# Attention's projections by halves of the heads, half of them between the heads; head norms' roots by Newton steps

## The chip, the cores and the metric

One core of one Trainium2 chip runs the whole program. The metric is the device time of one execution in microseconds (us). The engines are TensorE (PE in the rows; PEld is its weight load), VectorE (DVE), ScalarE (ACT), GpSimd (POOL) and SyncE (SP), which here only issues DMAs. TensorE's clock has two levels, 1.2 and 2.4 GHz; the rows give the granted clock as a share of the higher one.

## The reference, cut to what matters

Two layers over 256 latent and 256 context tokens of width 1024. Layer 0 is a gated convolution and a dense SwiGLU. Layer 1, where the change is, is differential attention and then 8 experts.

```python
q, k, v = split(a @ w_qkv, 3)          # latent tokens; the context needs only k and v
q = rms_norm(q.reshape(.., 16, 64), q_g); k = rms_norm(k.reshape(.., 16, 64), k_g)
q, k = rope_2d(q), rope_2d(k)          # latent tokens alone; context without rope
p = softmax(q @ k.T / 8)               # 16 half-heads, keys: latent and context
w = p[:, 0] - lam * p[:, 1]            # pairs of half-heads: 8 heads
o = rms_norm(w @ v, sub_g) * (1 - lam_init)
h = h + g1 * (o @ w_out)               # then the experts
```

## The kernel before, in words

**Matrix products.** Values are fp32. Each operand is split into a high and a low part (`hi`, `lo`), and a product is three TensorE matmuls (`mm3`: hi by hi, hi by lo, lo by hi). Tokens lie in four blocks of 128: blocks 0 and 1 are latent, 2 and 3 context. The activations' parts are `ah[k]` and `al[k]`, k = 0 to 7 over the depth of 1024.

**Weights.** They come by DMA in units of 1 MB (128 x 2048, four k steps of 512 columns each) into three raw buffers (`rw`, class `Loads`). Class `Parts` turns a unit into its parts: a cast on ScalarE (`wh`), then a subtraction on VectorE (`wl`). There are three slots for parts. `pump` converts what has arrived as long as a slot is free; `release` and `give` free the slots of units that are used up, and convert the next. 512 columns of the three matrices (two units) are numbered n: 0 and 1 are q, 2 and 3 are k, 4 and 5 are v. The even n are heads 0 to 3, the odd ones heads 4 to 7.

**Order.** Nothing is scheduled by a compiler: each engine works its instructions in the order in which the program issues them. What stands behind a waiting instruction on its engine waits too.

**Projections.** `group(n, pr, ws, new)` makes the 512 columns n for two token blocks (2pr and 2pr+1) in turns: at each of eight k steps one product (three matmuls) for the one block, one for the other. q needs one group, k and v two each. The first q group (n = 0) lies at the end of layer 0; in its midst stands `then()`, which reads the last mean, and `modulate`, which makes `ah` and `al` of the context blocks. Then `order` runs n = 1, 2, 3 and 4, that is all of q and k and half of v. Between the products of a group stands the head norm of the group before: `qk_norm` (square on ScalarE, sum per half-head on VectorE as `qr`, square root on ScalarE, reciprocal on VectorE, then the scaling `qx`, and rope in `qz` and `qy`), `qk_end` (the sum of the rope's parts), and `flip` (four transposes on TensorE into a PSUM bank, copied by ScalarE to `qT` or `kT`). `rows` makes three further rows that the end of the layer needs. Two banks of PSUM hold a group, and seven are there in all.

**Attention.** Sixteen steps m, one for each pair of a head and a latent block (`heads16`; before: block 0 with heads 0 to 7, then block 1). A step has `scores` (two matmuls into `sc`), `top` (the maxima `mx` on VectorE), `soft` (two exponentials `e` on ScalarE), for head m-1 `weigh` (VectorE, `zr` and `e`), for m-2 `turn` (four transposes into the one bank of `psw`, the tile `wt`, copied by ScalarE to `wT`), for m-3 `value` (four matmuls into `o`; the rows count each matmul of `scores` and `value` twice). With the first six heads `filler` runs the other half of v (n = 5), three k steps a head, two products each, in the two banks of `psf` (tile `mm`). Behind head 6 the slots of the weights are set free, and memory that is done with is given to further weights (`held.close`, pool `more`). `subnorm(t, ..)` and `sub_t(t, ..)` norm and transpose block t's outputs, and `outp` multiplies them with `w_out`; block 0 does so at steps 11 to 18, and block 1 after the loop.

Of the kernel before, what the change touches and what calls it, by code (L numbers as in the profile page):

```python
# [13 lines left out]
BF16 = mybir.dt.bfloat16  # L14
AF = mybir.ActivationFunctionType
# [4 lines left out]
P = 128  # L20
# [109 lines left out]
def backbone(ctx: ExitStack, tc: tile.TileContext, i, out, stage=9):  # L130
# [17 lines left out]
    units = [i["w0"][u] for u in range(49)] + [i["w1"][u] for u in range(16)]  # L148
# [475 lines left out]
    def group(n, pr, ws, new):  # L624

        ps = [new() for _ in range(2)]
        for k in range(KT):
            if len(ws) == k // 4:
                ws.append(parts.unit())
            wh, wl = ws[k // 4]  # L630
            c = slice(k % 4 * T2, (k % 4 + 1) * T2)
            for p, t in zip(ps, (2 * pr, 2 * pr + 1)):
                tk = slice(t * P, (t + 1) * P)
                mm3(p, ah[k][:, tk], al[k][:, tk], wh[:, c], wl[:, c], k == 0, k == KT - 1)
            yield ps

    for k, q0 in enumerate(group(0, 0, [], bank)):
        if k == 1:
            parts.pump(1)
        elif k == 2:  # L640
            jobs = then()
        elif k == 5:
            parts.give(1)
            modulate(jobs)
# [22 lines left out]
    pq = proj.enter_context(tc.tile_pool(name="qkv", bufs=1, side="right", reuse_waits="tile"))  # L667
# [4 lines left out]
    def qk_norm(ps, t, is_k):  # L672
        sq = pq.tile([P, T2], F32, name="qsq")
        A.activation(sq, ps, AF.Square)
        r = sm.tile([P, 8], F32, name="qr")
        V.tensor_reduce(r, heads(sq), axis=AX.X, op=OP.add)
        A.activation(r, r, AF.Sqrt, bias=eps, scale=1.0 / 64)
        V.reciprocal(r, r)
        x = pq.tile([P, T2], F32, name="qx", bufs=4)
        V.tensor_tensor(out=heads(x), in0=heads(ps), in1=r[:, :, None].to_broadcast([P, 8, 64]), op=OP.mult)  # L680
        if t >= 2:
            V.tensor_tensor(out=heads(x), in0=heads(x), in1=qkg[:, None, 64:].to_broadcast([P, 8, 64]), op=OP.mult)
            return x
        z = pq.tile([P, T2], F32, name="qz", bufs=2)
        xs = x.rearrange("p (h r b j) -> p h r b j", h=8, r=2, b=2)
        zs = z.rearrange("p (h r b j) -> p h r b j", h=8, r=2, b=2)
        rp = rope[:, is_k, 1, t].rearrange("p (r b j) -> p r b j", r=2, b=2)
        for r2 in range(2):
            for b in range(2):
                V.tensor_tensor(out=zs[:, :, r2, b], in0=xs[:, :, r2, 1 - b],  # L690
                                 in1=rp[:, None, r2, b].to_broadcast([P, 8, 16]), op=OP.mult)
        y = pq.tile([P, T2], F32, name="qy", bufs=2)
        V.tensor_tensor(out=heads(y), in0=heads(x), in1=rope[:, is_k, 0, t, None].to_broadcast([P, 8, 64]), op=OP.mult)
        return x, y, z

    def qk_end(a):
        if isinstance(a, tuple):
            x, y, z = a
            V.tensor_tensor(out=x, in0=y, in1=z, op=OP.add)
            return x  # L700
        return a

    def flip(x, t, dst):
        pt = bank()
        for j in range(4):
            PE.transpose(pt[:, j * P:(j + 1) * P], x[:, j * P:(j + 1) * P], ident)
        A.copy(dst[:, :, t * P:(t + 1) * P], pt.rearrange("p (n t) -> p n t", n=4))

# [28 lines left out]
    order = [(1, 0), (2, 0), (2, 1), (3, 0), (3, 1), (4, 0), (4, 1)]  # L737
    prev, flips, extra = (0, 0, q0), deque(), rows()
    ws = []
    for n, pr in order:  # L740
        if pr == 0:
            parts.release()
            parts.holding = n > 1
            ws = []
        xs = []
        for k, ps in enumerate(group(n, pr, ws, bank)):
            pn_, ppr, pps = prev
            if pn_ < 4:
                if k in (1, 2):
                    xs.append(qk_norm(pps[k - 1], 2 * ppr + k - 1, pn_ > 1))  # L750
                elif k in (3, 4):
                    xs[k - 3] = qk_end(xs[k - 3])
                    flips.append((xs[k - 3], 2 * ppr + k - 3, qT[pn_] if pn_ < 2 else kT[pn_ - 2]))
            elif k in (1, 2):
                A.copy(vv[pn_ - 4][2 * ppr + k - 1], pps[k - 1])
            if k > 5 and (len(flips) > 2 or pr and n == 4):
                flip(*flips.popleft())
            if k == 5 and pr:
                parts.give(1)
            if k in (3, 5) and n > 1:  # L760
                next(extra, None)
        prev = n, pr, ps
    for t in range(2):
        A.copy(vv[0][2 + t], ps[t])
    proj.close()
# [7 lines left out]
    onh, onl = (aw.tile([P, 2, 8, P], F32R, name=f"on{n}") for n in range(2))  # L773
# [3 lines left out]
    heads16 = [(h, t) for t in range(2) for h in range(8)]  # L777
# [74 lines left out]
    def filler():  # L852
        parts.release(1)
        parts.holding = True
        ws = []
        for pr in range(2):
            for k, ps in enumerate(group(5, pr, ws, lambda: psf.tile([P, T2], F32, name="mm"))):
                if k == 2:
                    parts.pump(1)
                yield  # L860
            for t in range(2):
                A.copy(vv[1][2 * pr + t], ps[t])

# [24 lines left out]
    fill, zs = filler(), {}  # L888
    out0 = None
    more = ExitStack()  # L890
    for m in range(19):
        if m < 16:
            scores(m)
        if 0 <= m - 3:
            value(m - 3)
        if 0 <= m - 2 < 16:
            turn(m - 2)
# [6 lines left out]
        if m < 6:  # L904
            for _ in range(3 if m < 5 else 2):
                next(fill, None)
        if m == 6:
            parts.release(1)
            held.close()
            pm = more.enter_context(tc.tile_pool(name="more", bufs=1, reuse_waits="tile"))  # L910
            parts.free.extend(part_slots(pm, 1, "x"))
            parts.last_use, xlo = parts.free[-1]
            parts.holding = True
            nh, nl = ([pm.tile([P, D], F32R, name=n), parts.last_use[:, c * D:(c + 1) * D]] for c, n in enumerate(("nh", "nl")))
            small = routing(pm)
            oh = [pm.tile([P, 2, P], F32R, name=f"oh{t}") for t in range(2)]
        if m in (7, 8, 9):
            parts.pump(1)
        if m == 11:
            subnorm(0, 0, 8)  # L920
        if m == 13:
            sub_t(0, 0, 4)
        if m == 14:
            sub_t(0, 4, 8)
        if m == 14:
            wo = [parts.unit() for _ in range(4)]
            out0 = [psf.tile([P, T2], F32, name="mm") for _ in range(2)]
        if m > 14:
            outp(out0, 0, m - 14 - 1)

        loads.free.extend({11: ada_slots[:1], 14: [flat], 15: ada_slots[1:] + later[:1], 18: later[1:]}.get(m, []))
# [5 lines left out]
    for h in range(18 - 14, 8):  # L937
# [398 lines left out]
```

## Time and profile before

| | |
|---|---|
| Median of 3 runs | 1669.6 us (1669.21 to 1669.99) |
| Profiled execution: its own time | 1667.59 us |
| Its span | 1665.3 us |
| TensorE busy | 1600.8 us, 96% of the span |
| VectorE, ScalarE, GpSimd busy | 80%, 53%, 1% |
| Layer 0 up to the first q | 0 to 612 us |
| q, k and half of v | 612 to 721 us |
| The sixteen heads | 721 to about 801 us |
| `subnorm`, output product, residual, routing | about 801 to 845 us |
| Experts | 845 to 1665 us |

Times in the trace count from the start of the span. A row of a timeline has the start, the time of one instruction (or of several alike that follow each other, with their count behind an x), engine, line, operation, what it writes and reads, and sizes. In square brackets stands how long the engine had been idle before it, and which engine's work ended that. For the matmuls the duration is modelled, so the distance of two starts says more than the duration of one.

### The profile page before, as it was taken

The numbers are of one execution on the slowest core, as the hardware profiler recorded it, in microseconds if no ns is written. First come the engines' busy times: TensorE is split into PE (matmuls) and PEld (weight loads), VectorE is DVE, ScalarE is ACT, GpSimd is POOL, SyncE is SP. The second block draws the span as 40 slices with busy tenths as digits, with TensorE's granted clock in tenths as the row PEclk, the third lists the DMA queues.
The fourth block names the chain that finished last, engine by engine and source line by source line (L and its number), as shares of the span: only waits on it lengthen the run. The fifth ranks groups of instructions, "written<-read, shape, count | busy, mean of one in ns | idle before, by whom it ended". The sixth has DMA issues, their size and how long they took to land. (4 is left out here: it accounts for less than half of the span.)

```text
span 1665.3 us, 20172 instructions
## 1 busy us (share of the span) xinstructions
PE 1600.8 (96%) x7415; PEld 1285.0 (77%) x7415; DVE 1328.9 (80%) x1886; ACT 885.5 (53%) x1241; POOL 13.1 (1%) x29
## 2 busy tenths in 40 slices
PE   8799899999999999997979999999999999999997
PEld 7587688888888887864768887888778887788886
DVE  5888887667658668536678898989989898998986
ACT  3222244222212244346557767777667776777774
POOL 0000000000001000000000000000000000000000
PEclk9999999999999999998979999999999999999999
DMA  9345534445547423212269988999889998899980
GB/s 357 106 175 199 186 109 167 152 149 180 177 165 273 168 84 119 102 51 101 102 237 361 366 331 324 350 350 374 313 336 356 356 346 323 331 365 348 357 339 28
DMA packets 55724, 400.30 MB, mean 240 GB/s; under 512 B 6449, under 2 KB 6481, under 8 KB 7105
## 3 DMA queue, kind: packets, MB, share of 16 engines
q1 hardware_dynamic: 55298, 398.50, 64.4%
q8 instruction: 60, 0.98, 0.2%
q0 software_dynamic: 320, 0.44, 0.2%
q14 instruction: 46, 0.38, 0.1%
HBM read 397.87 MB, written 1.05 MB: 240 GB/s over the span
## 5 line engine op out<-in xcount | busy, mean ns | idle before, releaser
L83 DVE TENSOR_TENSOR wl<-rw,wh 128x1024 fp32r<-128x1024 f32 (+1 forms) x211 | 321.9, 1561 | 98.1 <-ACT wh L79 97.6
L79 ACT CAST wh<-rw 128x1024 fp32r<-128x1024 f32 (+1 forms) x209 | 267.8, 1314 | 65.7 <-PE mm L174 57.4
L173 PE MATMUL mm<-ah,wh 128*128 128x512 f32 (+1 forms) x576 | 223.1, 387 | 7.9 <-ACT ah L313 7.3
L175 PE MATMUL mm<-ah,wl 128*128 128x512 f32 (+1 forms) x576 | 222.1, 386 | 5.0 <-DVE wl L83 5.0
L174 PE MATMUL mm<-al,wh 128*128 128x512 f32 (+1 forms) x576 | 222.4, 386 | 0.1
L253 DVE SCALAR_TENSOR_TENSOR junk<-ra,cb 128x1024 bf16<-128x1024 f32 x136 | 166.3, 1223 | 3.3
L175 PE MATMUL y<-wh,hl 128*128 128x512 f32 x352 | 141.6, 402 | 3.9 <-DVE hl L1132 3.8
L173 PE MATMUL h<-wh,xl 128*128 128x512 f32 x352 | 143.2, 407 | 0.0
L173 PE MATMUL h<-wh,xs 128*128 128x512 f32 x352 | 142.8, 406 | 0.0
L173 PE MATMUL y<-wh,hh 128*128 128x512 f32 x352 | 139.2, 395 | 0.5 <-ACT hh L1131 0.5
L174 PE MATMUL h<-wl,xs 128*128 128x512 f32 x352 | 139.2, 396 | 0.0
L174 PE MATMUL h<-wl,xl 128*128 128x512 f32 x352 | 139.1, 395 | 0.0
L175 PE MATMUL h<-wh,xl 128*128 128x512 f32 x352 | 139.0, 395 | 0.0
L174 PE MATMUL y<-wl,hh 128*128 128x512 f32 x352 | 138.9, 395 | 0.0
L175 PE MATMUL h<-wh,xs 128*128 128x512 f32 x352 | 138.8, 394 | 0.0
L173 PEld LDWEIGHTS mm<-ah,wh 128*128 128x128 f32 x576 | 109.6, 190 | 33.0 <-ACT ah L313 9.0
L175 PEld LDWEIGHTS mm<-ah,wl 128*128 128x128 f32 x576 | 109.6, 190 | 29.7 <-DVE wl L83 6.8
L174 PEld LDWEIGHTS mm<-al,wh 128*128 128x128 f32 x576 | 109.5, 190 | 23.8 <-DVE al L308 1.2
L83 DVE TENSOR_TENSOR wl<-ra,wh 128x1024 fp32r<-128x1024 f32 (+1 forms) x95 | 113.1, 1232 | 15.3 <-ACT wh L79 14.8
L83 DVE TENSOR_TENSOR wl<-rp,wh 128x1024 fp32r<-128x1024 f32 x96 | 112.7, 1221 | 6.4 <-ACT wh L79 6.4
L83 DVE TENSOR_TENSOR wl<-rq,wh 128x1024 fp32r<-128x1024 f32 x92 | 108.0, 1220 | 8.4 <-ACT wh L79 7.9
L79 ACT CAST wh<-rp 128x1024 fp32r<-128x1024 f32 x96 | 96.6, 1047 | 6.3 <-PE y L175 5.4
(278 smaller groups left out, 2961.2 us busy)
## 6 DMA issues: line engine op xcount, KB each, us to landing
rw<-moe SPq DMA_DIRECT2D x75, 1024.0 KB, 5.8
rw<-w SPq DMA_DIRECT2D x65, 1024.0 KB, 4.9
ra<-moe SPq DMA_DIRECT2D x48, 1024.0 KB, 6.1
rp<-moe SPq DMA_DIRECT2D x48, 1024.0 KB, 5.9
rq<-moe SPq DMA_DIRECT2D x46, 1024.0 KB, 6.4
ra<-ada SPq DMA_DIRECT2D x44, 1024.0 KB, 4.9
xl<-moe SPq DMA_DIRECT2D x24, 1024.0 KB, 6.3
xt<-moe SPq DMA_DIRECT2D x23, 1024.0 KB, 5.8
```

Of the source, the lines that this page charges most:

```text
L79: self.nc.scalar.copy(hi[:, c0], raw[:, c0])
L83: engine.tensor_tensor(out=lo[:, c], in0=raw[:, c], in1=hi[:, c].bitcast(F32), op=OP.subtract)
L173: PE.matmul(ps, wh, xh, start=first, stop=False)
L174: PE.matmul(ps, wh, xl, start=False, stop=False)
L175: PE.matmul(ps, wl, xh, start=False, stop=last)
L253: V.scalar_tensor_tensor(junk, raw[:, a * D:(a + 1) * D], 1.0, cb[:, s], op0=OP.mult, op1=OP.mult, accum_out=m[:, a, s:s + 1])
```

## The change

**Products one block at a time.** `project(n, ts, new)` takes the place of `group`: it runs all eight k steps of one token block, then those of the next. So a group's second weight unit is needed after four products.

**Halves of the heads.** The weight units come in the order n = 0, 2, 4, then 1, 3, 5. Before the attention run n = 0 (in the place of the old first group) and 2 and 4 (`projections((2, 4), bank, bank)`): q, k and v of heads 0 to 3. n = 1, 3 and 5 are `fill`, and `pull` runs eight of its products with each of the steps m = 0 to 9 (three behind `scores`, three behind `value`, two behind `turn`); what they write are the two banks of `psf`, and their transposes go through the one bank of `psw`. `heads16` now has heads 0 to 3 of both blocks, then 4 to 7 of both.

**Head norms.** `normed` is a generator that `follow` advances by one stage with each product. The root of the mean square is made without ScalarE: a first value comes from an integer operation on the bits (VectorE), and two Newton steps follow, eight small operations on GpSimd. Rope's `qz` is two instructions of 256 columns where it was four of 128.

**What stands elsewhere.** In a step `value` and `turn` now come behind `soft`. `held.close`, the release of slots and the pool `more` come at m = 10 (before, 6), the further conversions at 11 to 13 (before, 7 to 9), `subnorm(0)` at 14 (before, 11), both `sub_t(0)` at 15 (before, 13 and 14), and `outp` takes two heads a step from m = 16 (before, one from 15). Weight buffers go back to the loads at 7, 10, 15 and 18 (before, 11, 14, 15 and 18). In the first q, `modulate` moves ahead of `give(1)`, the conversion of the next unit.

```diff
-    units = [i["w0"][u] for u in range(49)] + [i["w1"][u] for u in range(16)]
+    units = [i["w0"][u] for u in range(49)] + [i["w1"][2 * n + u] for n in (0, 2, 4, 1, 3, 5, 6, 7) for u in range(2)]
...
+    after = deque()
+
+    def follow():
+        for a in list(after):
+            if next(a, after) is after:
+                after.remove(a)
+
+    def project(n, ts, new):
+
+        ws = []
+        for t in ts:
+            ps = new()
+            tk = slice(t * P, (t + 1) * P)
+            for k in range(KT):
+                if len(ws) == k // 4:
+                    ws.append(parts.unit())
+                wh, wl = ws[k // 4]
+                c = slice(k % 4 * T2, (k % 4 + 1) * T2)
+                mm3(ps, ah[k][:, tk], al[k][:, tk], wh[:, c], wl[:, c], k == 0, k == KT - 1)
+                if t == ts[0] and k == 2:
+                    parts.pump(1)
+                elif t == ts[-1] and k == 5:
+                    parts.give(1)
+                yield t, k, ps
+
+    q0 = {}
+    for t, k, q0[t] in project(0, (0, 1), bank):
+        if t == 0 and k == 4:
             jobs = then()
-        elif k == 5:
-            parts.give(1)
+        elif t == 1 and k == 3:
             modulate(jobs)
...
+    def normed(n, t, ps, new):
+
+        is_k = n // 2
         sq = pq.tile([P, T2], F32, name="qsq")
         A.activation(sq, ps, AF.Square)
-        r = sm.tile([P, 8], F32, name="qr")
-        V.tensor_reduce(r, heads(sq), axis=AX.X, op=OP.add)
-        A.activation(r, r, AF.Sqrt, bias=eps, scale=1.0 / 64)
-        V.reciprocal(r, r)
-        x = pq.tile([P, T2], F32, name="qx", bufs=4)
+        yield
+        r, m, e = (pq.tile([P, 8], F32, name=f"q{a}", bufs=2) for a in "rme")
+        V.tensor_reduce(m, heads(sq), axis=AX.X, op=OP.add)
+
+        V.tensor_scalar(m, m, 1.0 / 64, EPS, op0=OP.mult, op1=OP.add)
+        V.tensor_scalar(r.bitcast(I32), m.bitcast(I32), -0.5, float(0x5f1ffff9), op0=OP.mult, op1=OP.add)
+        for a, b in ((-0.703952253, 1.681915), (-0.5, 1.5)):
+            PO.tensor_tensor(out=e, in0=r, in1=r, op=OP.mult)
+            PO.tensor_tensor(out=e, in0=e, in1=m, op=OP.mult)
+            PO.tensor_scalar(e, e, a, b, op0=OP.mult, op1=OP.add)
+            PO.tensor_tensor(out=r, in0=r, in1=e, op=OP.mult)
+        for _ in range(4):
+            yield
+        x = pq.tile([P, T2], F32, name="qx", bufs=3)
         V.tensor_tensor(out=heads(x), in0=heads(ps), in1=r[:, :, None].to_broadcast([P, 8, 64]), op=OP.mult)
+        yield
...
+    def projections(ns, new, flips):
+
+        for n in ns:
+            ts = range(2 if n < 2 else 4)
+            parts.release(1)
+            parts.holding = True
+            for t, k, ps in project(n, ts, new):
+                follow()
+                if k == KT - 1:
+                    after.append(normed(n, t, ps, flips) if n < 4 else kept(n, t, ps))
+                yield
+        while after:
+            follow()
+            yield
...
-    heads16 = [(h, t) for t in range(2) for h in range(8)]
+    heads16 = [(4 * n + j, t) for n in range(2) for t in range(2) for j in range(4)]
...
     for m in range(19):
         if m < 16:
             scores(m)
-        if 0 <= m - 3:
-            value(m - 3)
-        if 0 <= m - 2 < 16:
-            turn(m - 2)
+        pull(3)
         if m < 16:
             mx = top(m)
         if 0 <= m - 1 < 16:
             weigh(m - 1, zs.pop(m - 1))
         if m < 16:
             zs[m] = soft(m, mx)
-        if m < 6:
-            for _ in range(3 if m < 5 else 2):
-                next(fill, None)
-        if m == 6:
+        if 0 <= m - 3:
+            value(m - 3)
+        pull(3)
+        if 0 <= m - 2 < 16:
+            turn(m - 2)
+        pull(2 if m < 10 else 99)
+        if m == 10:
             parts.release(1)
+            proj.close()
             held.close()
```

**First piece: ScalarE in the first q.** `wh_76` and `wh_78` are the casts of the next group's two weight units, `ah_264` to `ah_271` what `modulate` makes, `qsq` the square in the first head norm. Before:

```order
L79 CAST wh_76<-rw_72 128x2048
L313 ACTIVATE ah_264<-mt,mod_0_2508 128x256
L313 ACTIVATE ah_265<-mt,mod_1_2580 128x256
L313 ACTIVATE ah_266<-mt,mod_2_2652 128x256
L313 ACTIVATE ah_267<-mt,mod_3_2724 128x256
L313 ACTIVATE ah_268<-mt,mod_4_2796 128x256
L313 ACTIVATE ah_269<-mt,mod_5_2868 128x256
L313 ACTIVATE ah_270<-mt,mod_6_2940 128x256
L313 ACTIVATE ah_271<-mt,mod_7_3012 128x256
L79 CAST wh_78<-rw_73 128x2048
L674 ACTIVATE qsq<-mm 128x512
```

With the change, from the sixth `ah` on:

```order
L314 ACTIVATE ah_270<-mt,mod_6_2940 128x256
L314 ACTIVATE ah_271<-mt,mod_7_3012 128x256
L80 CAST wh_76<-rw_72 128x2048
L80 CAST wh_78<-rw_73 128x2048
L688 ACTIVATE qsq<-mm 128x512 x2
L760 COPY xt<-mm 128x512 x2
```

The cast of the first of the two units has moved from ahead of the eight `ah` to behind them.

**Second piece: VectorE at the first heads.** `wl` are subtractions of weight units, `mx` the maxima of a head and their negation, `zr` and `e` the weighing of a head; ahead of either piece stands the first unit's subtraction, `wl_75`. Before:

```order
L790 TENSOR_REDUCE mx<-sc 128x2
L791 TENSOR_SCALAR mx<-mx 128x2
L83 TENSOR_TENSOR wl_77<-rw_72,wh_76 128x2048
L790 TENSOR_REDUCE mx<-sc 128x2
L791 TENSOR_SCALAR mx<-mx 128x2
L807 RECIPROCAL zr<-z_5107 128x1
L808 SCALAR_TENSOR_TENSOR zr<-z_5099,nlam,zr 128x1
L809 SCALAR_TENSOR_TENSOR e<-e,zr 128x512
```

With the change:

```order
L803 TENSOR_REDUCE mx<-sc 128x2
L804 TENSOR_SCALAR mx<-mx 128x2
L691 TENSOR_REDUCE qm<-qsq 128x8
L693 TENSOR_SCALAR qm<-qm 128x8
L694 TENSOR_SCALAR qr<-qm 128x8
L803 TENSOR_REDUCE mx<-sc 128x2
L804 TENSOR_SCALAR mx<-mx 128x2
L820 RECIPROCAL zr<-z_4889 128x1
L821 SCALAR_TENSOR_TENSOR zr<-z_4868,nlam,zr 128x1
L822 SCALAR_TENSOR_TENSOR e<-e,zr 128x512
L84 TENSOR_TENSOR wl_77<-rw_72,wh_76 128x2048
L703 TENSOR_TENSOR qx<-mm,qr 128x512
```

Between the first two heads' maxima now stands the start of a head norm (`qm`, `qr`), and the second unit's subtraction stands behind the second head's maxima, ahead of the scaling `qx`.

**Third piece: ScalarE at the first heads.** `e` are the exponentials (two a head), `wT` the copy of a head's transposed weights, `rp_4400` the copy of a transposed `qx`. Before, from the second unit's cast on:

```order
L79 CAST wh_76<-rw_72 128x2048
L799 ACTIVATE e,z_5099<-sc,mx 128x512
L799 ACTIVATE e,z_5144<-sc,mx 128x512
L816 COPY wT<-wt 128x512
L799 ACTIVATE e,z_5099<-sc,mx 128x512
L799 ACTIVATE e,z_5183<-sc,mx 128x512
```

With the change, from the second head's exponentials on:

```order
L812 ACTIVATE e,z_4868<-sc,mx 128x512
L812 ACTIVATE e,z_4944<-sc,mx 128x512
L80 CAST wh_76<-rw_72 128x2048
L80 CAST wh_78<-rw_73 128x2048
L688 ACTIVATE qsq<-mm 128x512
L812 ACTIVATE e,z_4868<-sc,mx 128x512
L812 ACTIVATE e,z_5013<-sc,mx 128x512
L724 COPY rp_4400<-wt 128x4x128
L829 COPY wT<-wt 128x512
```

Two casts now stand ahead of the third head's exponentials, and the copy out of the first `wt` (a transposed `qx`) behind them.

## Rows read from the trace of the kernel before

**Rows 1.** the page, part 1: busy us, share of the span, instructions

```profile
PE 1600.8 (96%) x7415; PEld 1285.0 (77%) x7415; DVE 1328.9 (80%) x1886; ACT 885.5 (53%) x1241; POOL 13.1 (1%) x29
```

**Rows 2.** windows; columns: window, length, busy us of five engines, clock, DMA share, GB/s

```profile
612.00:721.00 109.00, 103.89 (x488) 83.89 (x488) 74.10 (x126) 47.62 (x72) 0.00 (x0) 0.98 0.30 105
721.00:755.25 34.25, 34.20 (x160) 23.36 (x156) 15.74 (x28) 15.52 (x41) 1.37 (x6) 1.00 0.10 36
755.25:801.84 46.59, 35.15 (x170) 20.96 (x169) 32.97 (x56) 30.74 (x86) 0.00 (x0) 0.82 0.32 114
```

**Rows 3.** TensorE's timeline: start us, duration us, operation [idle before <-releaser]

```profile
612.03 0.39 PE L173 MATMUL mm<-wh,ah 128*128 128x512 f32 x1
...
612.72 0.40 PE L173 MATMUL mm<-wh,ah 128*128 128x512 f32 x1
...
619.61 0.50 PE L174 MATMUL mm<-wl,ah 128*128 128x512 f32 x1 [1.18 <-DVE wl L83]
```

**Rows 4.** VectorE's timeline in the first q, same columns

```profile
617.27 4.49 DVE L83 TENSOR_TENSOR wl<-rw,wh 128x2048 fp32r<-128x2048 f32 x2 [1.36 <-ACT wh L79]
621.68 1.75 DVE L300 RECIPROCAL rs<-rs 128x256 f32<-128x256 f32 x1
...
625.48 1.26 DVE L312 SCALAR_TENSOR_TENSOR mt<-xc,mod,rs 128x256 f32<-128x256 f32 x3
```

**Rows 5.** ScalarE's timeline in the first q

```profile
615.35 3.68 ACT L79 CAST wh<-rw 128x2048 fp32r<-128x2048 f32 x2
...
630.74 0.51 ACT L313 ACTIVATE ah<-mt,mod 128x256 fp32r<-128x256 f32 x1 [0.28 <-DVE mt L312]
```

**Rows 6.** TensorE's timeline, waits of the window up to 721

```profile
645.08 0.51 PE L174 MATMUL mm<-wl,ah 128*128 128x512 f32 x1 [1.95 <-DVE wl L83]
...
652.72 0.65 PE L706 MATMUL mm<-ident,qx 128*128 128x128 f32 x4 [0.82 <-ACT xt L724]
...
720.63 1.13 PE L786 MATMUL sc<-ra,rp 64*128 64x512 f32 x4 [1.16 <-ACT xl L764]
```

**Rows 7.** VectorE's timeline, head norm of the first q

```profile
635.29 0.68 DVE L676 TENSOR_REDUCE qr<-qsq 128x8 f32<-128x512 f32 x1
...
636.58 0.69 DVE L680 TENSOR_TENSOR qx<-mm,qr 128x512 f32<-128x512 f32 x1
637.30 0.90 DVE L690 TENSOR_TENSOR qz<-qx,rope 128x128 f32<-128x128 f32 x4
638.11 0.69 DVE L693 TENSOR_TENSOR qy<-qx,rope 128x512 f32<-128x512 f32 x1
```

**Rows 8.** GpSimd's timeline, layer 0

```profile
508.27 1.21 POOL L731 TENSOR_SCALAR wrg<-wr,mod 128x8 f32<-128x8 f32 x1 [8.24 <-DVE mod L244]
511.12 0.31 POOL L731 TENSOR_SCALAR wrg<-wr,mod 128x8 f32<-128x8 f32 x1 [1.64 <-DVE mod L244]
```

**Rows 9.** VectorE's timeline at the same place

```profile
508.10 1.22 DVE L253 SCALAR_TENSOR_TENSOR junk<-ra,cb 128x1024 bf16<-128x1024 f32 x1
```

**Rows 10.** VectorE's timeline, maxima of a head

```profile
732.70 1.23 DVE L790 TENSOR_REDUCE mx<-sc 128x2 f32<-128x1024 f32 x1
```

**Rows 11.** ScalarE's timeline, first head and a cast

```profile
723.33 1.28 ACT L799 ACT_TABLE_LOAD   x1 [2.27 <-DVE mx L791]
724.63 0.69 ACT L799 ACTIVATE e<-sc,mx 128x512 f32<-128x512 f32 x1
...
725.97 1.90 ACT L79 CAST wh<-rw 128x2048 fp32r<-128x2048 f32 x1
```

**Rows 12.** TensorE's timeline, a head without products, and a wait

```profile
755.25 1.13 PE L786 MATMUL sc<-ra,rp 64*128 64x512 f32 x4
756.31 1.16 PE L822 MATMUL o<-xl,wT 128*128 128x128 f32 x8
...
757.84 1.13 PE L786 MATMUL sc<-ra,rp 64*128 64x512 f32 x4
...
762.68 1.16 PE L822 MATMUL o<-rp,wT 128*128 128x128 f32 x8 [1.12 <-ACT wT L816]
```

## What the change will do to the time: a prediction

> **What bounds the kernel now.** I read the page first: TensorE is busy 96% of the span [rows 1], so only time in which it waits, or runs at its lower clock, can be won or lost. The windows show where that is near the change [rows 2]. From 612 to 721 us (all q and k, half of v, behind each other) 109.0 us hold 103.9 busy and the granted clock is 0.98. From 721 to 755 (heads 0 to 5 with the other half of v between them) TensorE is busy 34.20 of 34.25. From 755.25 to 801.84 (heads 6 to 15 with nothing between) it is busy 35.2 of 46.6 at a granted clock of 0.82, between its levels of 1.2 and 2.4 GHz. A head costs TensorE 2.59 when nothing stops it (scores, value, turn: from one scores to the next [rows 12]); ten of them and the first two groups of transposes of `sub_t` make about 27, so 19.5 of these 46.6 us are lost. The expert stage behind 845 is untouched, and it has its own weights' pace; I cost it at nothing: its loads wait for buffers, which the change frees no later (heads 7 and 10 instead of 11 and 14), and were they late, TensorE would wait there by as much.
>
> **What the change moves.** Products, transposes and head steps stay the same in number; only their order and the roots differ. So I lay out TensorE's waits in three stretches, with 0.70 for a product (three matmuls: the first starts at 612.03, the next product's at 612.72 [rows 3]).
>
> *q of the first half and the start of k.* Before, the two token blocks of q alternate, so the fifth step needs the second weight unit after eight products; now it needs it after four, at 612.03 + 4 x 0.70 = 614.8. That unit is cast by ScalarE from 615.35 on [rows 5], behind work that stays, and VectorE's subtractions of two units start at 617.27 and take 4.49 together [rows 4]; the first is there at 619.5, as before, where TensorE waited 1.18 for it [rows 3]. Now it waits 619.5 - 614.8 = 4.7 (less one matmul, 0.23). Twelve products and the mean's matmul later q ends at about 628.1, and k's fifth product comes at 628.1 + 4 x 0.70 = 630.9. Its weights now stand behind `modulate` on both engines (first order piece). VectorE's reciprocal stays at 621.68; without the subtraction that stood between, `modulate` starts at 623.4 instead of 625.48 [rows 4], so ScalarE's last `ah`, which ended at 631.25 [rows 5], ends at 629.1; cast 1.9 to 631.0, subtraction 2.2 to 633.2. TensorE waits 2.3, less 0.23. Together 4.5 + 2.1 = 6.6 against 1.2 before: **5.4 lost**. A bound below is 3.3, the first wait alone, if the second were hidden; above, a stretch at the lower clock behind either wait. Before, after a wait of 1.95 at 645.08 the window as a whole shows 0.98, 2% of 109 or 2.2 us [rows 2, 6].
>
> *The rest of k and v, up to the first scores.* VectorE takes 0.7 for the reduction with its small operations near 0.4 more, 0.72 for the product `qx`, 0.8 for four pieces of `qz` (now two of twice the size; I take 0.7), 1.3 for `qy` (0.69) and the sum together [rows 7]. Between reduction and `qx` stand eight GpSimd operations that each wait for the last. The trace has GpSimd's tensor_scalar on 128x8 at 0.31 and at 1.21 [rows 8]; so eight are 2.5 to 9.7, and I take 3.0 (0.31 each, half a us for the hand-overs), since VectorE mostly stands still waiting for them. Before, square root and reciprocal took 636.58 less 635.97, when the reduction ends: 0.6. Starting with the subtraction at 633.2, then 635.4 for the next unit, the first block is: reduced 636.5, roots 639.6, `qx` 640.4, `qz` 641.1, the next reduction 642.2, sum 643.5. TensorE reaches its transposes at 641.0 and waits 2.5. In the same way the second block's sum comes at 648.7 against 647.5 (1.2). The two context blocks of k stand behind weight subtractions and come 1.2 and 1.6 late; the scores' bank adds 0.5. That is 7.0, against 1.95 + 0.82 + 1.16 [rows 6] and 2.0 of low clock before: **1.1 lost**. With GpSimd at 2.5 it is a gain of 1, with 9.7 beside every VectorE operation a loss of 15.
>
> *Heads 0 to 9 with the second half's products.* Count from the first scores, at 0. ScalarE casts the first unit of k when v's last product ends, 0.5 to 2.4; VectorE subtracts to 4.6 and only then takes head 0's maxima (1.23 and their negation, 1.3 [rows 10]) to 5.9, since they stand behind it (second piece). Table load 1.28, exponentials 1.34 [rows 11] to 8.6; square of q's block 9.1; reduced 10.25; head 1's maxima 11.55, its exponentials 12.95; only then the cast of k's second unit, 14.85, the subtraction 17.05, `qx` 17.7 (all in the order of the pieces). TensorE has two banks for products; the third block needs the bank that this `qx` reads. It arrives there at 3 x 1.06 + 16 x 0.70 = 14.4 and waits 3.3. Behind `qx` VectorE does `qz`, `qy`, the sum, one more subtraction (21.9), a reduction and head 2's maxima (24.2); the exponentials end at 25.6. ScalarE's copy of the transposed `qx` stands behind them (third piece), at 26.2, and the one `psw` bank holds both it and head 0's `turn`, which TensorE reaches at 22.3: 3.9 more. From head 3 on VectorE's load per head (2.5 for the head, 4.0 for a norm, about 1 for GpSimd) is under TensorE's 2.59 + 8 x 0.70 + 0.4 = 8.6, and nothing waits. **7.2 lost**, where before lost 0.05. If the first half of this chain were hidden, 3.9; with a stretch of low clock, 9.5.
>
> *Heads 10 to 15 and the way out.* Four heads fewer lie bare. But what stops these heads before is lumps of VectorE and ScalarE work: weight conversions, and the root of `subnorm` with its table loads. Of them, three conversions and the root stay in the bare part; one goes, and with it the 1.1 that it cost [rows 12]. If the loss fell with the number of heads it would be 4/10 of 19.5 = 7.8. I take **1 gained**, near the count by lumps, and keep 7.8 for the range.
>
> **Sum.** 5.4 + 1.1 + 7.2 - 1 = 12.7 on the profiled execution's own 1667.59: 1680.3. The runs' median, 1669.6, is 2.0 above that execution, so the forecast is 1682.3, slower by 0.8%.
>
> A behaviour weighed against the trace: GpSimd's operations at 1.21 lie beside VectorE's product of 1.22 with two SBUF inputs, which starts at 508.10 [rows 9]; the one at 0.31 lies beside none such. The Trainium skill, "GPSIMD Engine Reference", section 8 (Key points), says that GpSimd shares its SBUF interfaces with VectorE and contends with instructions that have two SBUF inputs; the rows agree. By that rule every step of the roots beside a `wl`, `qz` or `qy` would take that operation's length, which is the third rival.
>
> **Rivals.**
> *Faster.* The filled heads hold, and the bare part shrinks with its heads: 7.8 gained against q's first wait alone (3.3): 1669.6 - 4.5 = 1665. For it: before, filled heads lost 0.05 [rows 2]. Against it: VectorE then had 2.5 us of work a head in 5 to 7 us, and one subtraction; now heads 1 and 2 have two subtractions and two norms. It decides if the waits of the first heads together stay under 4 us.
> *The same.* The waits in q and at the first heads come as said (3.3 and 3.9) and the bare part gives all 7.8 back: 1669.6 - 0.6 = 1669.
> *GpSimd starved.* Two or three of eight operations in each of six norms before the scores last as VectorE's do, 0.9 more each: 13 on top, 1695. Against it: VectorE waits for the roots itself and then leaves the ports alone.
>
> **How the numbers follow.** Forecast 0.58 (its own range 1673 to 1691), GpSimd starved 0.12, the same 0.12, faster 0.18. 0.2% is 3.3 us, about what a measurement of this kernel can tell from no change. So slower 0.70, same 0.12, faster 0.18. The range from 1666 to 1696 takes in the same, half of the starved case, and leaves out most of the faster one.
>
> **What would show it.** After the change TensorE should show a wait of about 4.5 for `wl` in q, near 614.8, and one of 2 in k near 631; waits of `mm` for `qx` by transposes up to 2.5 us until 690; the first scores near 690; a product waiting 3 us for VectorE some 14 us behind them and a `wt` waiting 4 us for ScalarE at about 22; then no wait for seven heads; and a bare part of 35 to 38 us. GpSimd's rows should be at 0.3, few at 0.7 and more. I am wrong if the casts overtake, if GpSimd's chain takes 10 us, or if the bare part falls under 32.

## The result: 1.1% slower

The changed kernel takes 1687.1 us (median of 4 runs, 1686.6 to 1687.4) against 1669.4 of the kernel before in the same comparison: 1.0108 times as long, with a 95% interval of 1.0090 to 1.0125. The forecast was 1682.3 with a range of 1666 to 1696. The span of its profiled execution is 1685.6 us, 20.3 more than before. TensorE is on balance busy as long as before ([rows 1]), and idle for 85.5 us instead of 64.5; part 1 of the page:

```profile
PE 1600.1 (95%) x7415; PEld 1287.5 (76%) x7415; DVE 1329.8 (79%) x1882; ACT 884.4 (52%) x1229; POOL 34.8 (2%) x125
```

The windows of the changed kernel, cut at the first q, the first scores, the scores of head 10 (the first without products) and the second routing product (columns as in [rows 2]):

```profile
608.58:686.08 77.50, 68.06 (x318) 53.75 (x316) 46.17 (x76) 31.17 (x44) 15.01 (x56) 0.98 0.23 82
686.08:779.62 93.54, 85.11 (x393) 60.24 (x393) 55.42 (x96) 42.71 (x91) 14.09 (x54) 0.96 0.23 79
779.62:865.62 86.00, 59.70 (x292) 44.93 (x291) 48.60 (x91) 37.55 (x86) 0.00 (x0) 0.80 0.30 111
865.62:1685.60 819.98, 804.53 (x3651) 645.39 (x3650) 732.38 (x903) 593.71 (x785) 0.00 (x0) 0.99 0.85 327
```

The kernel before has the same four landmarks at 612.03, 720.63, 755.25 (head 6) and 846.06:

```profile
612.03:720.63 108.60, 103.49 (x487) 83.56 (x485) 74.07 (x126) 47.22 (x72) 0.00 (x0) 0.98 0.30 104
720.63:755.25 34.62, 34.58 (x160) 23.66 (x160) 15.74 (x28) 15.88 (x41) 1.37 (x6) 1.00 0.11 40
755.25:846.06 90.81, 70.41 (x356) 49.57 (x356) 59.31 (x111) 49.66 (x123) 0.00 (x0) 0.84 0.32 117
```

To compare stretch by stretch, what the change moves from one to the next has to be moved in the old numbers too: 48 products of 0.70 and six groups of transposes of 0.4 from the first stretch to the second, four heads of 2.59 from the third to the second. So regrouped, 108.60, 34.62 and 90.81 become 72.60, 80.98 and 80.45. The changed kernel has 77.50, 93.54 and 86.00: **4.9, 12.6 and 5.5 us lost**. Two more differences lie outside: the first q comes 3.4 us sooner, though no instruction ahead of it has changed, and the experts take 0.7 longer. 4.9 + 12.6 + 5.5 - 3.4 + 0.7 = 20.3, the difference of the spans.

TensorE's waits in the three stretches, from its timeline:

```profile
613.73 0.50 PE L174 MATMUL mm<-wh,ah 128*128 128x512 f32 x1 [2.20 <-ACT wh L80]
616.06 0.79 PE L175 MATMUL mm<-wl,ah 128*128 128x512 f32 x1 [1.83 <-DVE wl L84]
...
639.90 0.63 PE L723 MATMUL mm<-ident,qx 128*128 128x128 f32 x4 [1.39 <-DVE qx L717]
...
703.66 0.47 PE L174 MATMUL mm<-wh,ah 128*128 128x512 f32 x1 [2.73 <-DVE qx L703]
...
712.25 0.66 PE L827 MATMUL wt<-ident,e 128*128 128x128 f32 x4 [2.16 <-ACT rp L724]
...
743.40 0.50 PE L174 MATMUL mm<-wh,ah 128*128 128x512 f32 x1 [1.61 <-DVE qx L703]
...
751.11 0.66 PE L827 MATMUL wt<-ident,e 128*128 128x128 f32 x4 [1.92 <-ACT ra L724]
...
784.72 1.16 PE L835 MATMUL o<-rp,wT 128*128 128x128 f32 x8 [1.39 <-ACT wT L829]
...
790.63 2.08 PE L835 MATMUL o<-rp,wT 128*128 128x128 f32 x8 [3.25 <-ACT wT L829]
...
798.53 2.08 PE L835 MATMUL o<-rp,wT 128*128 128x128 f32 x8 [2.97 <-ACT wT L829]
...
815.52 1.12 PE L853 MATMUL wt<-ident,xf 128*128 128x128 f32 x4 [6.48 <-ACT wT L829]
```

The reader should see three things. The waits of the first q (2.20 and 1.83, where before one of 1.18 stood, [rows 3]) and for `qx` are those that were forecast. At the first heads a product waits 2.73 for `qx` and a `wt` 2.16 for ScalarE's copy, as forecast; but the same pair, 1.61 and 1.92, comes again 40 us later. And from head 11 on TensorE waits for nearly every `wT` copy of ScalarE, up to 6.48, where before its longest waits (2.79, 2.50 and 1.98) were for VectorE's `e`, two of them in these rows of the kernel before:

```profile
766.63 1.09 PE L814 MATMUL wt<-ident,e 128*128 128x128 f32 x4 [2.79 <-DVE e L809]
...
779.47 0.83 PE L814 MATMUL wt<-ident,e 128*128 128x128 f32 x3 [2.50 <-DVE e L809]
```

Behind some of these waits the granted clock falls to the lower level, and a product's matmul then takes 0.43 from start to start instead of 0.23, as from 705.13 to 707.69 behind the 2.73 (granted clock 0.51). Behind the 2.16 and the 1.61 it stays at 1.00. In the third stretch `o` takes 2.08 instead of 1.16 behind the 3.25 and the 2.97, and the window shows a clock of 0.80.

GpSimd's eight steps at a place where VectorE waits for them, first and last, and one step beside VectorE's weighing:

```profile
633.74 0.20 POOL L696 TENSOR_TENSOR qe<-qr 128x8 f32<-128x8 f32 x1 [438.55 <-DVE qr L694]
...
635.71 0.20 POOL L699 TENSOR_TENSOR qr<-qr,qe 128x8 f32<-128x8 f32 x1
...
697.73 0.69 POOL L698 TENSOR_SCALAR qe<-qe 128x8 f32<-128x8 f32 x1
```

```profile
697.61 0.75 DVE L822 SCALAR_TENSOR_TENSOR e<-e,zr 128x512 f32<-128x512 f32 x1
```

The first chain takes 635.91 - 633.74 = 2.2 us. The step at 697.73 takes 0.69 where its fellows take 0.20; it lies beside the weighing `e`, a product of VectorE with two SBUF inputs, and ends with it. That is the sharing of SBUF interfaces of which the Trainium skill speaks ("GPSIMD Engine Reference", section 8, Key points); the trace agrees. But of the 96 steps of the twelve norms 11 take 0.44 or more, one in each norm among the heads, and the rival of a starved GpSimd did not come.

### The profile page after: what moved, and what is told of

Read it like the earlier page. It is cut to its first block, busy times and chain, and to the rows that moved or that the text cites. A ratio compares the mean times of both kernels' runs of the same rounds, so it can differ in the third digit from the quotient of the medians.

```text
span 1685.6 us, 20266 instructions
## 1 busy us (share of the span) xinstructions
PE 1600.1 (95%) x7415; PEld 1287.5 (76%) x7415; DVE 1329.8 (79%) x1882; ACT 884.4 (52%) x1229; POOL 34.8 (2%) x125
```

## The experiments

Twelve kernels ran. All stretches, in us (starts are those of the four landmarks in TensorE's timeline; kernels in the old order are regrouped as above):

| kernel | first q at | to first scores | heads with products | on to routing | rest |
|---|---|---|---|---|---|
| before | 612.0 | 72.6 | 81.0 | 80.5 | 819.2 |
| changed | 608.6 | 77.5 | 93.5 | 86.0 | 820.0 |
| 1, old order in the bare heads | 608.2 | 77.5 | 93.5 | 76.4 | 819.3 |
| 2, before with the new order | 612.2 | 72.6 | 81.5 | 93.1 | 819.4 |
| 3, roots on ScalarE | 608.4 | 73.6 | 103.1 | 85.3 | 819.7 |
| 4, q in turns | 608.4 | 80.2 | 93.5 | 85.2 | 819.8 |
| 5, as 1, `qx` earlier | 608.3 | 77.5 | 96.1 | 77.2 | 819.1 |
| 6, as 1, flips earlier | 608.4 | 77.6 | 86.4 | 78.7 | 819.5 |
| 7, as 1, roots mixed | 608.1 | 73.7 | 94.3 | 78.8 | 819.6 |
| 8, as 1, with 5, 6 and 7 | 608.1 | 73.6 | 84.8 | 78.4 | 819.5 |
| 9, before, `qr` elsewhere | 608.4 | 72.6 | 81.0 | 82.7 | 819.7 |
| 10, as 8, without 5 | 608.3 | 75.2 | 87.3 | 77.2 | 819.2 |
| 11, as 8, Newton steps in `subnorm` | 608.5 | 73.6 | 84.8 | 78.0 | 819.6 |
| 12, as 8, last products spread | 608.2 | 73.7 | 81.3 | 81.5 | 819.5 |

Each row is one execution. The stretch on to routing differs by 2 us between executions with the same instructions in it (before and 9), and the stretch to the first scores by 1.5 (8 and 10: in 10 the granted clock was 0.89 from 640 to 655 us, where no wait stands, and in 8 it was 1.00); less than that says nothing there. In 12 the five products of head 10 lie in the stretch on to routing.

**1. The old order in the bare heads.** In the changed kernel, from head 10 on:

```diff
         pull(3)
+        if m >= 10:
+            value(m - 3)
+            if m - 2 < 16:
+                turn(m - 2)
         if m < 16:
             mx = top(m)
...
-        if 0 <= m - 3:
+        if 0 <= m - 3 and m < 10:
             value(m - 3)
         pull(3)
-        if 0 <= m - 2 < 16:
+        if 0 <= m - 2 and m < 10:
             turn(m - 2)
```

> The changed kernel, but from head 10 on, where no products are left, value and turn stand ahead of the maxima and the exponentials again, as before. Theory A (on ScalarE the copy of the turned weights wT now stands behind this head's exponentials, and so behind its maxima; with no products between, TensorE waits for it in every bare head): the bare heads at TensorE's pace go from 4.05 us back to 2.6 where no lump of VectorE stands, the waits for wT of 1.39, 3.25, 2.97, 1.30 and 6.48 shrink by half or more, and the time falls by 5 to 8 us, to 1679 to 1682. Theory B (the lumps alone, that is weight conversions and the root with its table loads, set the bare part): the time stays within 1.5 us of 1687.

1677.9 us, 1.0058 times the kernel before (1.0044 to 1.0072): the excess falls from 1.08% to 0.58%, a little more than was expected, and the whole of it lies in the stretch on to routing, 9.6 us shorter. ScalarE's timeline in two bare heads of the changed kernel, and of this one:

```profile
782.32 0.69 ACT L812 ACTIVATE e<-sc,mx 128x512 f32<-128x512 f32 x1 [2.01 <-DVE zr L820]
...
784.05 0.61 ACT L829 COPY wT<-wt 128x512 f32<-128x512 f32 x1
788.23 0.69 ACT L812 ACTIVATE e<-sc,mx 128x512 f32<-128x512 f32 x1 [3.56 <-DVE zr L820]
...
789.96 0.61 ACT L829 COPY wT<-wt 128x512 f32<-128x512 f32 x1
```

```profile
781.95 0.60 ACT L829 COPY wT<-wt 128x512 f32<-128x512 f32 x1
782.43 0.71 ACT L812 ACTIVATE e<-sc,mx 128x512 f32<-128x512 f32 x1
...
784.53 0.60 ACT L829 COPY wT<-wt 128x512 f32<-128x512 f32 x1
787.77 0.69 ACT L812 ACTIVATE e<-sc,mx 128x512 f32<-128x512 f32 x1 [2.64 <-DVE mx L804]
```

In the changed kernel each copy `wT` follows the two exponentials `e` of the same step, and these wait (2.01, 3.56) for VectorE's maxima (the rows name `zr`, which stands right behind them). With the old order the copy stands ahead: at 784.53, and the wait of 2.64 that follows holds up the exponentials alone. The next `value` needs the copy, not the exponentials. TensorE's waits for `wT` in the bare heads are gone; the longest that is left is 3.06, for VectorE.

**2. The new order in the kernel before.** The mirror image:

```diff
-        if 0 <= m - 3:
-            value(m - 3)
-        if 0 <= m - 2 < 16:
-            turn(m - 2)
...
             zs[m] = soft(m, mx)
+        if 0 <= m - 3:
+            value(m - 3)
+        if 0 <= m - 2 < 16:
+            turn(m - 2)
```

> The kernel before with one edit: value and turn stand behind the exponentials in every head, as in the changed kernel. Theory A (order of the copy behind the exponentials): heads 0 to 5 with their products show nothing, the ten bare heads lose about 1.3 us each less what the lumps already cost, so 6 to 12 us, 1675 to 1681. Theory B (the lumps set it): 1668 to 1671.

1681.2 us, 1.0078 (1.0064 to 1.0092), a little more than the upper end of what was expected. The windows of heads 0 to 5 and of the bare heads, and two of TensorE's waits:

```profile
720.76:755.92 35.16, 34.57 (x160) 23.70 (x160) 15.74 (x28) 15.26 (x38) 1.37 (x6) 1.00 0.12 41
755.92:859.42 103.50, 71.05 (x355) 51.60 (x355) 59.46 (x111) 50.06 (x126) 0.00 (x0) 0.81 0.29 103
```

```profile
768.93 2.07 PE L822 MATMUL o<-rp,wT 128*128 128x128 f32 x8 [5.25 <-ACT wT L816]
...
782.74 1.65 PE L822 MATMUL o<-rp,wT 128*128 128x128 f32 x6 [5.25 <-ACT wT L816]
```

Six heads with products go from 34.6 to 35.2 us; the rest from 90.8 to 103.5. So the order costs next to nothing while TensorE has products, and over 1 us in each head where it has none. Where VectorE has a lump it waits 5.25 at once, and the clock falls behind it.

**3. Roots on ScalarE.**

```diff
-        V.tensor_scalar(m, m, 1.0 / 64, EPS, op0=OP.mult, op1=OP.add)
-        V.tensor_scalar(r.bitcast(I32), m.bitcast(I32), -0.5, float(0x5f1ffff9), op0=OP.mult, op1=OP.add)
-        for a, b in ((-0.703952253, 1.681915), (-0.5, 1.5)):
...
+        A.activation(r, m, AF.Sqrt, bias=eps, scale=1.0 / 64)
+        V.reciprocal(r, r)
```

> The changed kernel with the roots as before: square root on ScalarE, reciprocal on VectorE, in the place of eight GpSimd operations and two small ones of VectorE. Theory A (the roots matter little): up to the first scores the waits of the transposes for qx (1.39, 0.48, 1.23, 0.65) lose 2 in sum, and with the heads each of six norms loads ScalarE's table twice, 2.6 us, beside the exponentials, which adds 0 to 5 us to the waits there; in all 1685 to 1691. Theory B (GpSimd's chain is what made the changed kernel slow): 8 us or more faster, 1679 or less.

1692.5 us, 1.0147 (1.0131 to 1.0162), over the upper end of what was expected. Ahead of the first scores it is 3.9 us shorter, where 2 were expected, and with the heads 9.6 longer, where 0 to 5 were. ScalarE's timeline around the first two roots among the heads:

```profile
691.52 1.28 ACT L693 ACT_TABLE_LOAD   x1
692.82 0.30 ACT L693 ACTIVATE qr<-qm,eps 128x8 f32<-128x8 f32 x1
...
701.57 1.28 ACT L693 ACT_TABLE_LOAD   x1
707.13 0.30 ACT L693 ACTIVATE qr<-qm,eps 128x8 f32<-128x8 f32 x1 [4.28 <-DVE qm L691]
709.04 1.28 ACT L807 ACT_TABLE_LOAD   x1 [1.61 <-DVE zr L815]
```

A root among the heads needs its table loaded and the exponentials' table again behind it, 1.28 each, and ScalarE stands in between until VectorE's sum is there (4.28). The Trainium skill ("ScalarE: Activation LUTs", section "What ACT_TABLE_LOAD costs") gives a switch 2.66 us, load and drain; the rows here show the load's 1.28, and the root starts 1.30 after the load (692.82 behind 691.52), so here the measured 1.3 stands. So Newton steps were worth 9.6 us among the heads and cost 3.9 ahead of them.

**4. The first q in turns.** `project(0, ..)` is replaced by the old group, with `then`, `pump`, `give` and `modulate` where they stood.

```diff
-    q0 = {}
-    for t, k, q0[t] in project(0, (0, 1), bank):
-        if t == 0 and k == 4:
...
+    for k in range(KT):
...
+        for t in range(2):
...
+            mm3(ps[t], ah[k][:, tk], al[k][:, tk], wh[:, c], wl[:, c], k == 0, k == KT - 1)
+        if k == 1:
+            parts.pump(1)
+        elif k == 2:
             jobs = then()
-        elif t == 1 and k == 3:
+        elif k == 5:
+            parts.give(1)
             modulate(jobs)
```

> The changed kernel with the first q's products in turns for the two token blocks again, with the mean, the conversions and modulate where they stood before. Theory A (the second weight unit is needed after four products): the waits of 2.20, 1.83 and 0.99 become one of 1.2, and the stretch at the lower clock behind them goes; 4 to 6 us faster, 1681 to 1683. Theory B (what is saved there is waited for again in k, behind the weights and the norms): within 1.5 us of 1687.

1686.8 us, 1.0110 (1.0094 to 1.0125): nothing won. TensorE's timeline:

```profile
615.84 0.50 PE L175 MATMUL mm<-wl,ah 128*128 128x512 f32 x1 [1.06 <-DVE wl L84]
...
633.36 0.66 PE L771 MATMUL mm<-ident,xl 128*128 128x128 f32 x4 [2.18 <-ACT xt L772]
...
638.95 1.09 PE L735 MATMUL mm<-ident,qx 128*128 128x128 f32 x4 [3.92 <-DVE qx L729]
```

The wait in q is one of 1.06, as expected, but TensorE now waits 2.18 for a copy of `xt` and 3.92 for the first `qx`. VectorE's sum that makes this `qx`, here and in the changed kernel, and the windows behind the wait, in the same order:

```profile
638.11 0.69 DVE L729 TENSOR_TENSOR qx<-qy,qz 128x512 f32<-128x512 f32 x1
...
639.07 0.69 DVE L717 TENSOR_TENSOR qx<-qy,qz 128x512 f32<-128x512 f32 x1
```

```profile
638.95:655.00 16.05, 16.05 (x81) 13.81 (x82) 9.97 (x21) 4.03 (x8) 9.03 (x30) 0.82 0.01 2
639.90:655.00 15.10, 14.62 (x86) 12.43 (x86) 10.67 (x22) 4.20 (x8) 9.00 (x30) 1.00 0.01 2
```

Counted from the first q, the sum starts 29.8 us behind it in turns and 30.5 in the changed kernel: `modulate`, the weights' cast and subtraction and the norm, one behind the other, set it, and the order of TensorE's products hardly moves it. What TensorE no longer waits in q it waits here, and behind the longer wait the clock is 0.82 and not 1.00. Theory A fell. This execution is 2 us longer than the three others of this kernel, so the 80.2 of the table is high.

**5. `qx` earlier among the heads.** On the kernel of 1, one `yield` less ahead of `qx`, one more ahead of the transposes:

```diff
-        for _ in range(4):
+        for _ in range(4 if new is bank else 3):
             yield
         x = pq.tile([P, T2], F32, name="qx", bufs=3)
...
-        for _ in range(5):
+        for _ in range(5 if new is bank else 6):
             yield
```

> The first experiment's kernel (value and turn ahead of the exponentials from head 10 on, 1677.9) and in it, for the norms among the heads alone, the scaling qx one product earlier, that is ahead of the conversions that stand behind the sixth product of a group's last block; the transposes stay where they were. Theory A (the products' bank is held by a qx that stands behind a weight subtraction on VectorE): the waits of 2.74 and 1.63 go, with the lower clock behind the first (about 1.6), and it gives 4 to 6 us, 1672 to 1674. Theory B (the norm itself, GpSimd's eight steps included, is late): the waits stay above 1.5 each and the time within 1.5 of 1677.9.

1679.4 us, 1.0060 (1.0047 to 1.0074), no gain: the waits went as theory A said, and the time stayed as theory B said. The products' waits of 2.74 and 1.63 are gone, but the next wait has grown, from 2.16 to 5.19:

```profile
711.23 1.11 PE L827 MATMUL wt<-ident,e 128*128 128x128 f32 x4 [5.19 <-ACT rp L724]
...
752.17 1.11 PE L827 MATMUL wt<-ident,e 128*128 128x128 f32 x4 [2.88 <-ACT ra L724]
```

**6. Flips earlier among the heads.** On the kernel of 1:

```diff
-        for _ in range(5):
+        for _ in range(5 if new is bank else 3):
             yield
         dst = kT[n - 2] if is_k else qT[n]
```

> The first experiment's kernel and in it, for the norms among the heads alone, the transposes of qx two products earlier, so that ScalarE's copy out of the one bank wt stands ahead of the head's exponentials and not behind them. Theory A (that order makes turn wait): the waits of 2.16 and 1.91 for ScalarE go; where the sum of the rope is late, at the lumps, TensorE waits up to 2 for it instead; 2 to 5 us faster, 1673 to 1676. Theory B (the copy is late for another reason): within 1.5 of 1677.9.

1671.9 us, 1.0014 (1.0005 to 1.0023), some 7 us faster than 1, over what was expected. Its heads with products:

```profile
685.99:772.34 86.35, 82.34 (x393) 60.03 (x393) 55.23 (x96) 42.31 (x91) 14.11 (x54) 0.98 0.26 86
```

93.5 became 86.4 and the clock went from 0.96 to 0.98. The transposed `qx` now leaves the one bank `wt` ahead of the head's exponentials, so no `turn` waits for it. The products' waits for `qx` stay, at 2.73 and 1.28.

**7. Roots mixed.** On the kernel of 1, ScalarE's root where `new is bank`, Newton steps otherwise.

> The first experiment's kernel with ScalarE's square root and VectorE's reciprocal in the norms ahead of the first scores, and the Newton steps in those among the heads. With roots on ScalarE throughout, the stretch from the first q to the first scores was 73.6 instead of 77.5 us, and the heads with products 103.1 instead of 93.5. Theory A (each root has its place: Newton costs 2.3 us of waiting where VectorE has nothing else, and spares table loads beside the exponentials): 3.9 us faster, 1674. Theory B (the first heads take up what was won ahead of them): within 1.5 of 1677.9.

1675.9 us, 1.0037 (1.0023 to 1.0050), 3.5 us faster than 1 by the ratios. The stretch to the first scores takes 73.7, as in experiment 3 (73.6), and the first heads give back 0.8.

**8 and 10. All four repairs, and all but the earlier `qx`.**

> Four repairs together: value and turn ahead of the exponentials from head 10 on, flips among the heads two products earlier, roots on ScalarE ahead of the first scores and Newton steps behind, and the scaling qx among the heads one product earlier. The last gave nothing by itself (1.6 to 2.6 us more at turn, behind the exponentials, for 4.4 fewer at the product's bank); with the copies out of wt no longer behind the exponentials, theory A (the two waits of a lump are one chain, and the first repair only moved it) has it give 2 to 3 us here. Sum: 1672 - 3.9 - 2.5 = 1665 to 1667, 3 us under the kernel before. Theory B (VectorE's lump itself sets the heads, whichever product waits): the same as the next kernel within 1 us.

> The last one without the scaling's earlier place. Theory A: the heads with products 86.4 us as with the early flips alone, 73.7 ahead of them, so 3.5 to 4 us under the 1672 of the early flips: 1668. If the first heads take up what is won ahead of them (theory B), 1670 or more.

1666.4 us, 0.9984 (0.9975 to 0.9993), and 1668.6, 0.9993 (0.9984 to 1.0002). By the medians of eleven runs each `qx` earlier is worth some 2 us once the flips are out of the way (the intervals of the ratios overlap; the heads with products took 84.8 against 87.3 in one execution each), where alone it was worth nothing. That is theory A, a chain whose second wait had hidden the first. The windows of 8:

```profile
608.09:681.73 73.64, 68.39 (x319) 55.11 (x317) 44.30 (x70) 31.64 (x48) 0.00 (x0) 0.95 0.25 86
681.73:766.49 84.76, 81.20 (x393) 58.81 (x392) 55.94 (x96) 42.87 (x92) 14.03 (x54) 1.00 0.25 87
766.49:844.92 78.43, 56.80 (x292) 42.99 (x291) 48.57 (x91) 37.47 (x86) 0.00 (x0) 0.84 0.32 122
```

**9. The kernel before with a small tile elsewhere.** No instruction and no order changes; all that lies behind the pool `sm` in memory, `ah` and `al` among it, lies 64 bytes lower (two buffers of 32 bytes a partition), as in the changed kernel:

```diff
-        r = sm.tile([P, 8], F32, name="qr")
+        r = pq.tile([P, 8], F32, name="qr", bufs=2)
```

> The kernel before with one edit: the norm's small tile qr lies in the pool qkv and not in the pool sm, so that everything behind sm, ah and al among it, lies 64 bytes lower, as in the changed kernel; no instruction and no order changes. Theory A (the 3.4 us by which the changed kernel reaches the first q sooner come from where ah and al lie): a matmul of 512 columns in layer 0 starts every 0.229 to 0.231 us instead of 0.2334, the first q starts near 608.5 instead of 612.0, and the time falls by 3 to 4 us, to 1665. Theory B (it is chance between executions): 612 and 1668 to 1669.

1665.9 us, 0.9981 (0.9972 to 0.9990). The same 250 us of layer 0 in the kernel before, the changed one and this one:

```profile
300.00:550.00 250.00, 250.00 (x1074) 201.55 (x1073) 170.55 (x266) 62.84 (x57) 6.06 (x8) 1.00 0.53 189
```

```profile
300.00:550.00 250.00, 250.00 (x1087) 203.83 (x1086) 173.59 (x271) 63.55 (x57) 0.00 (x0) 1.00 0.54 192
```

```profile
300.00:550.00 250.00, 250.00 (x1088) 203.82 (x1087) 173.58 (x271) 63.44 (x57) 6.08 (x8) 1.00 0.54 192
```

TensorE is busy throughout in all three at a granted clock of 1.00, but gets through 1074, 1087 and 1088 matmuls. The first q starts at 608.4.

**11 and 12. Two further steps on the kernel of 8**: Newton steps for the root in `subnorm` too; and the last sixteen products spread over heads 8 to 10 (`pull` gives six, five and five), so that five heads are bare, and the release of the slots one head later.

> The four repairs, and the roots of the output's norm by the same two Newton steps on GpSimd as well, so that ScalarE loads no square-root table beside the last heads' exponentials. Theory A (two table loads of 1.28 stand in the last heads' exponentials and in the way of the transposes behind): the last heads give 1 to 3 us against the kernel of the four repairs. Theory B (there VectorE's work and its wait for eight GpSimd steps, 2.3 us, are as long as ScalarE's wait of 2.0): within 1 us of it.

> The four repairs, with the last sixteen products of the second half's v spread over heads 8, 9 and 10 (six, five and five, where they were eight, eight and none), so that five heads instead of six have no products; the release of the slots and what follows it one head later. Theory A (what a head without products loses is that TensorE has nothing to do while VectorE works off a lump): one bare head fewer, and its lump now beside products, 1 to 3 us faster than the four repairs' 1666.4. Theory B (the lumps stay in the heads that are bare, since they wait for the same release of slots, and the loss goes with the lumps): within 1 us of it.

1666.6 us (0.9987, 0.9978 to 0.9996) and 1666.8 (0.9990, 0.9982 to 0.9999): neither can be told from 8. In 11 the transposes' first wait for the normed outputs fell from 2.55 to 1.58, and the stretch on to routing by 0.4, less than executions differ. In 12 one bare head fewer gave way to another wait, of 2.86 for a `wT` at head 11; why the sum stays the same is not shown.

## Why the forecast held, and where it failed

Direction and range held; the time is 4.8 us above the forecast, and that is the sum of larger errors of both signs. That it is no more is in part luck. Between the two profiled executions, for which the sum was made, 19.7 us lie (1687.29 less 1667.59), where the sum has 12.7; that error would be 3.4 larger without a gain in layer 0 that no term had, and it is 2.2 smaller between the medians, since the median lay 2.0 above the profiled execution before and 0.2 below it after.

- **q and the start of k, and the rest up to the first scores** (5.4 and 1.1 lost, 6.5 together): 4.9 measured. The wait in q was 4.0 for 4.5; k's second unit 0.99 for 2.1, since TensorE came there 2.0 later, most of it by the lower clock behind the waits in q. The waits for `qx` were 1.39 and 0.48 for 2.5 and 1.2: at the first TensorE came 1.0 later than forecast, and at the second `qx` was ready 0.7 sooner, since eight GpSimd steps took 2.2 us and not 3.0. Experiment 4 shows that the wait in q has no price of its own: with q in turns, TensorE waits for VectorE's chain at the norm instead.
- **Heads 0 to 9** (7.2 lost): 12.6 measured. The two waits of the first heads were right in cause, and they ended where the forecast had them (17.6 and 26.2 us behind the first scores, for 17.7 and 26.2); they were smaller (2.73 and 2.16 for 3.3 and 3.9) since TensorE came to them later. The step that failed is that from head 3 on "nothing waits": it counted work per head and forgot that the units change again between k and v, at head 6, where 1.61 and 1.92 are waited. The four waits make 8.4 of the 12.6. The rest, some 4, is the lower clock behind them (0.96 over the stretch), kept for the range only. Experiments 5, 6 and 8 show the mechanism: one chain of a subtraction, `qx`, exponentials and copy.
- **Heads 10 to 15** (1 gained): 5.5 lost. The bare part, up to the first output product, took 42.0 us where the forecast named 35 to 38. The failed step is that the bare part's loss goes with VectorE's and ScalarE's lumps alone. That `value` and `turn` now stand behind `soft` was noted as part of the change and costed at nothing, with no cover named; the cover is the products, and the bare heads have none. Experiments 1 and 2 show it, 9.6 us one way and 12.7 the other. With the old order the bare part takes 33.7 and the term would have been 4.1 gained, of which 2 may be the difference between executions.
- **What no term had**: the 3.4 us of layer 0. Experiment 9 shows that it comes with the 64 bytes, not with the order.
- **The rivals.** Faster, and the same, needed a bare part that gives 7.8 back; as written it lost 5.5. With the repairs of 8 the change ends 3 us under the kernel before, which is what the 64 bytes alone give it (9). So halves of the heads, repaired, neither gain nor lose, as far as these runs can tell. That GpSimd starves did not happen: 11 of 96 steps took 0.44 to 0.69 instead of 0.20.

What stays open is why 64 bytes matter, and which of the tiles that lie behind `sm` it is: no run varied the addresses of `ah`, `al` and the weights one by one.

## What to carry to other kernels

When instructions move behind others on an in-order engine, ask at every place of the loop what covers them: an order that costs nothing under products cost 10 us where these had run out. Follow a chain past its first wait before repairing it, since the second can be waiting behind it. And when a change shifts memory, run the old order with the new layout as well, or the layout's share is credited to the order.

## What the runs showed of the hardware

A matmul of 128 x 512 in layer 0 took 250 / 1074 = 0.233 us from start to start with all that lies behind `sm` at the old addresses and 250 / 1088 = 0.230 with it 64 bytes lower, at a granted clock of 1.00 in both, and ahead of the first q that adds up to 3.4 to 3.6 us. A small GpSimd operation (128 x 8) took 0.20 us, a dependent one following 0.28 after the last one's start, and 0.69 beside a VectorE operation with two SBUF inputs.
